# Merging the delta rule's block inverses in four steps of the pumped chain instead of one

## The chip, the cores and the metric

The kernel runs on one core of a Trainium2 chip. The metric is the device time of one execution in microseconds, the median of several runs. Five engines work side by side, each through its own queue in order: TensorE (PE in the profile; its weight loads are PEld), VectorE (DVE), ScalarE (ACT), GpSimd (POOL) and SyncE (SP), which here issues weight loads. A semaphore tells one engine that another is done.

## The reference, cut to what matters

A decoder trunk of two layers on x of 256 x 2048, fp32. Layer 0 is a gated DeltaNet with 16 heads of 128 x 128, layer 1 is differential attention; each ends with a squared-ReLU MLP, and each sub-layer with a layer norm. The part that the change touches is the chunked delta rule:

```python
lower = where(strict, einsum('bhnid,bhnjd->bhnij', k_beta, k) * decay, 0.0)
tri = lower + eye(CHUNK)
rhs = concatenate([v * beta, k_beta * exp(g)], -1)
sol = triangular_solve(tri, rhs, lower=True, unit_diagonal=True)
...
o = rms_norm(o, norm_w) * silu(z)
return o @ w_out
```

The kernel takes a chunk of 128 rows in place of 64, which gives the same function: two tiles t = 0, 1 of 128 rows for the 256 positions. Each (head, tile) has a triangular matrix of 128 x 128 whose inverse is applied to a right-hand side.

## The kernel before, in words

Nearly all of the time goes into gemms with streamed weights. `gemm` puts a gemm of 256 x K by K x 1024 into a plan; `run` goes through the plan in steps of SC = 4 weight tiles. In a step, for both row tiles t, every weight tile takes part in `product`: three 128x512 matmuls (L174, L175, L176) for high times high, high times low and low times high parts of fp32 numbers, for each of the two column groups. I call these the dense products; their tile is `acc`. `load_weights` fetches the tiles of the next step (L159, on SyncE's queue), and `split` makes the high part on ScalarE (L78) and the low part on VectorE (L79).

Small work is laid between the dense products. After each t of a step `pump` emits one item of the list `chain` and `rate` items (here 2) of the list `units`. `drain` empties both at once; the second gate gemm calls it at its last step, since the output projection behind it needs the whole delta rule. A scheduler then places the emitted instructions on the engines' queues by dependencies and buffers, so an engine's order is not quite the order of emission. Pools bound what can be under way: 11 buffers `blk` (128 x 2048), 8 buffers `sm` (128 x 512), and in PSUM 4 `acc` and 4 `ps`.

The delta rule runs in two halves of 8 heads. For each half there are gemms for k, q and v, then for both halves two gate gemms. Of a half:

- `score` (four items, two heads each): decay rows on VectorE (L525, L526), cumulative sums and k·k, q·k products on TensorE (L530 to L535, L550, L551), exponentials on ScalarE (L538, L539), causal selection on GpSimd (L541), products on VectorE (L553, L554). It leaves U1, A1 and UA2.
- the chain of `start_inverse`: `inv_gather` collects the 64 diagonal blocks of 32 x 32 through DRAM, three items that do nothing (rests), six items `inv_rows` with VectorE's forward substitution (L580, L587), `inv_scatter` (L589) sends the inverses back through DRAM into Z, two rests, `inv_flip` turns the blocks on VectorE (L601) into Y, a rest, and `inv_merge` (L603).
- `inv_merge` builds the inverse of 128 x 128 out of those of 32 x 32: for two 32-blocks at (0, 32) and at (64, 96), then for two 64-blocks, a lower product U·Z (L617), a copy on ScalarE (L618), the product with Y (L621) and a negated eviction to Y on VectorE (L622); for the first pair the turned product (L628) and an eviction to Z (L629) as well. A group is 16 matmuls of 32x32, or 8 of 64x64 for eight of the 16 matrices. All of it is one item of the chain.
- `solve` (two items, four heads each, put into the chain by `start_solve` when v is done): products with the inverse and U1 on TensorE (L642, L647, L651), copies on ScalarE (L643, L652), a subtraction on VectorE (L648), the output (L657, L659), its norm with small operations on VectorE (L665 to L671, `rsqrt` L85 to L89), and the scaled output `st["o"]` (L672).

The evacuation of a gate gemm, `ev` of `gate`, applies tanh on ScalarE, multiplies on VectorE (L738) and multiplies by `st["o"]` (L739); `to_features` then transposes it on TensorE (L204) as input of the output projection.

Of the kernel before, what the change touches and what calls it, by code (L numbers as in the profile page):

```python
# [14 lines left out]
ALU = mybir.AluOpType  # L15
# [3 lines left out]
P = 128  # L19
# [6 lines left out]
G = 512  # L26
# [9 lines left out]
class Trunk:  # L36
# [178 lines left out]
    @staticmethod  # L215
    def cols(w, c0, r0=0):
        return lambda k: w[r0 + k * P : r0 + (k + 1) * P, c0 : c0 + C]
# [96 lines left out]
    @staticmethod  # L314
    def ends(n):

        return [5, 5, 6] if n == D // C - 1 else None
# [47 lines left out]
    def gated_deltanet(self, x, w_in, conv_w, a_log, dt_bias, norm_w, w_out, g, b, out=None):  # L365
# [6 lines left out]
        nc = self.nc  # L372
        v_ = nc.vector
        NH, DK, HH = 16, 128, 8
# [198 lines left out]
        def inv_rows(hf, j0, j1):  # L573
            Gp = hf["inv"][:64, :C].rearrange("p (j i) -> p j i", j=32)
            X = hf["inv"][:64, C:].rearrange("p (i c) -> p i c", i=32)
            for j in range(j0, j1):
                n = 31 - j
                t0 = j % 2 * 256
                t = hf["t"][:64, t0 : t0 + n * (j + 1)].rearrange("p (i c) -> p i c", i=n)
                v_.tensor_tensor(  # L580
                    t,
                    Gp[:, j, j + 1 :].unsqueeze(2).broadcast_to([64, n, j + 1]),
                    X[:, j : j + 1, : j + 1].broadcast_to([64, n, j + 1]),
                    op=ALU.mult,
                )
                xs = X[:, j + 1 :, : j + 1]
                v_.tensor_tensor(xs, xs, t, op=ALU.subtract)  # L587

        def inv_scatter(hf):  # L589
            X = hf["inv"][:64, C:].rearrange("p (i c) -> p i c", i=32)  # L590
            hf["Z"] = self.blk()
            nc.gpsimd.memset(hf["Z"], 0.0)
            Zv = hf["Z"].rearrange("p (n c) -> p n c", c=P)
            buf = self.dram.tile([4, 2 * HH, 32, 32], F32, name="g_inverses")
# [4 lines left out]
        def inv_flip(hf):  # L599
            hf["Y"] = self.blk()  # L600
            v_.transpose(hf["Y"], hf["Z"])  # L601

        def inv_merge(hf):  # L603

            Z = hf["Z"].rearrange("p (n c) -> p n c", c=P)
            Y = hf["Y"].rearrange("p (n c) -> p n c", c=P)
            U = lambda n: hf["U1"][:, n] if n < HH else hf["UA2"][:, 0, n - HH]
            mm = nc.tensor.matmul
            for w, r0 in ((32, 0), (32, 64), (64, 0)):
                a, b_ = slice(r0, r0 + w), slice(r0 + w, r0 + 2 * w)  # L610
                per = G // w
                for n0 in range(0, 2 * HH, per):
                    N = range(n0, n0 + per)
                    cs = lambda n: slice((n - n0) * w, (n - n0 + 1) * w)
                    tp, ts = self.ps(), self.sm()
                    for n in N:
                        mm(tp[b_, cs(n)], U(n)[a, b_], Z[a, n, a], start=True, stop=True)  # L617
                    nc.scalar.copy(ts[b_], tp[b_])  # L618
                    yp = self.ps()
                    for n in N:  # L620
                        mm(yp[a, cs(n)], ts[b_, cs(n)], Y[b_, n, b_], start=True, stop=True)  # L621
                    v_.tensor_scalar(  # L622
                        Y[a, n0 : n0 + per, b_], yp[a].rearrange("p (n c) -> p n c", c=w), -1.0, None, op0=ALU.mult
                    )
                    if w == 32 and r0 == 0:
                        zp = self.ps()
                        for n in N:
                            mm(zp[b_, cs(n)], Y[b_, n, b_], ts[b_, cs(n)], start=True, stop=True)  # L628
                        v_.tensor_scalar(  # L629
                            Z[b_, n0 : n0 + per, a], zp[b_].rearrange("p (n c) -> p n c", c=w), -1.0, None, op0=ALU.mult  # L630
                        )

        def solve(hf, gi, H):

            Y = hf["Y"].rearrange("p (n c) -> p n c", c=P)
            rv = hf["r"]
# [39 lines left out]
        def start_inverse(hf):  # L676
            rest = [(lambda *a: None, (hf,))]
            rows = [(lambda hf, j=j: inv_rows(hf, j, min(j + 6, 31)), (hf,)) for j in range(0, 31, 6)]
            self.chain.extend([(inv_gather, (hf,))] + rest * 3 + rows)
            self.chain.extend([(inv_scatter, (hf,))] + rest * 2 + [(inv_flip, (hf,))] + rest + [(inv_merge, (hf,))])  # L680

        def start_solve(hf, H):
            self.chain.extend((solve, (hf, g_, H)) for g_ in range(NG))
# [1 line left out]
        def half(hh):  # L685
            hf, H = {}, hh * HH

            def ev_for(name, ct):
# [15 lines left out]
                def follow():  # L704
                    if name == "v":
                        hf["r"] = self.blk().rearrange("p (t h d) -> p t h d", t=NT, h=HH)
                        for h in range(0, HH, 2):
                            self.later(v_unit, hf["raw"], h, ct, hf["r"], hf["rsc"])
                        if hh == 0:
                            st["o"] = [self.blk() for _ in range(NT)]  # L710
                        self.later(start_solve, hf, H)
                        return
                    hf[name] = self.blk().rearrange("p (h t) -> p h t", h=HH)
                    hf["S" + name] = self.small([NT, HH], "g_S" + name)
                    for h in range(0, HH, 2):
                        self.later(qk_unit, hf["raw"], h, ct, hf[name], hf["S" + name])
                    if name == "q":
                        self.later(scalars, hf, H)
                        for h in range(0, HH, 2):
                            self.later(score, hf, H, h)  # L720
                        self.later(start_inverse, hf)
# [232 lines left out]
```

## Time and profile before

| | us |
|---|---|
| median of 3 runs | 2472.16 |
| lowest and highest run | 2465.31, 2475.14 |
| profiled execution | 2465.03 |
| its span | 2463.3 |
| TensorE busy | 2416.1 (98%) |
| VectorE busy | 1497.2 (61%) |
| ScalarE busy | 1078.2 (44%) |
| GpSimd busy | 90.3 (4%) |
| mean granted clock of TensorE | 0.992 |

The profile is of one execution; L12 is line 12 of the kernel. Times in it are microseconds from the start of the span. A row of the timeline gives start, length, engine, line, operation, output and inputs, size and count, and in brackets how long the engine stood idle ahead of it and for whom. A view by stretches gives busy time and number of records of each engine in each stretch and the TensorE clock that was granted, 1.00 being full. Matmuls overlap, so what one takes from the next is the distance of two starts; an fp32 matmul outside the dense products makes two records.

### The profile page before, as it was taken

How to read it: one execution, taken by the hardware profiler on the slowest of the kernel's cores; microseconds unless marked ns; L12 is line 12 of the kernel's file. 1: busy time of each engine (PE TensorE's matmuls, PEld its weight loads, DVE VectorE, ACT ScalarE, POOL GpSimd, SP SyncE). 2: the span in 40 equal slices, each digit the busy share in tenths (PEclk: the TensorE clock that was granted, in tenths of full speed). 3: DMA queues.
4: the chain of work that ended last, by engine and by line, in shares of the span. 5: the costliest groups of instructions: out<-in, count | busy, mean ns of one | idle time of the engine just before them, and what ended most of it. 6: DMA issues, size and time to landing. Idle time of an engine off the chain costs nothing.

```text
span 2463.3 us, 30465 instructions
## 1 busy us (share of the span) xinstructions
PE 2416.1 (98%) x11492; PEld 1983.3 (81%) x11492; DVE 1497.2 (61%) x2333; ACT 1078.2 (44%) x1474; POOL 90.3 (4%) x94
## 2 busy tenths in 40 slices
PE   8999999998999999999998999999999999999997
PEld 7888888887888888888887878788788888888886
DVE  4789689667554544545557575665755554555556
ACT  4545345433443433434433464643443443443442
POOL 0010010002000000000002000000200000000001
PEclk9999899999999999999999999999999999999999
DMA  6545345564555556565554545455455555656553
GB/s 229 155 139 175 98 140 160 166 233 158 188 185 191 182 194 222 172 214 182 195 197 146 180 137 171 155 174 167 161 198 195 182 190 186 217 179 214 185 195 121
DMA packets 120211, 438.84 MB, mean 178 GB/s; under 512 B 13760, under 2 KB 13792, under 8 KB 119040
## 3 DMA queue, kind: packets, MB, share of 16 engines
q1 hardware_dynamic: 115920, 420.79, 52.0%
q0 software_dynamic: 2560, 11.13, 1.4%
q10 hardware_dynamic: 1584, 4.98, 0.5%
q8 instruction: 90, 1.47, 0.2%
q14 instruction: 57, 0.47, 0.1%
HBM read 433.70 MB, written 3.15 MB: 177 GB/s over the span
## 4 chain that ended last, share of the span: by engine, by line
PE 90%; DVE 6%; DMA 2%; issue 1%; ACT 1%; POOL 0%; ACTq 0%; POOLq 0%; DVEq 0%
PE acc L174 27%; PE acc L175 27%; PE acc L176 27%; PE ps L204 3%; DVE wl L79 1%; DVE blk L266 1%; DVE blk L265 1%; PE ps L819 1%; ACT wh L78 1%; PE ps L550 1%; DMA wr<-in_gdn_w_in_dram 1%; PE ps L485 1%; DMA wr<-in_mlp_w_up_dram 0%; PE ps L621 0%; PE ps L847 0%
## 5 line engine op out<-in xcount | busy, mean ns | idle before, releaser
L79 DVE TENSOR_TENSOR wl<-wr,wh 128x1024 fp32r<-128x1024 f32 x785 | 954.5, 1227 | 675.0 <-ACT wh L78 632.1
L78 ACT CAST wh<-wr 128x1024 fp32r<-128x1024 f32 x800 | 832.1, 1052 | 945.6 <-PE acc L176 757.2
L174 PE MATMUL acc<-wh,xhl 128*128 128x512 f32 x1920 | 764.3, 398 | 0.0
L175 PE MATMUL acc<-wl,xhl 128*128 128x512 f32 x1920 | 757.7, 395 | 3.2 <-POOL wl L79 3.2
L176 PE MATMUL acc<-wh,xhl 128*128 128x512 f32 x1920 | 754.8, 393 | 0.0
L174 PE MATMUL acc<-wh,blk 128*128 128x512 f32 x1280 | 500.0, 391 | 0.0
L176 PE MATMUL acc<-wh,blk 128*128 128x512 f32 x1280 | 499.4, 390 | 0.0
L175 PE MATMUL acc<-wl,blk 128*128 128x512 f32 x1280 | 499.1, 390 | 0.0
L175 PEld LDWEIGHTS acc<-wl,xhl 128*128 128x128 f32 x1920 | 363.7, 189 | 75.7 <-POOL wl L79 4.4
L174 PEld LDWEIGHTS acc<-wh,xhl 128*128 128x128 f32 x1920 | 363.8, 189 | 73.8 <-issue 1.7
L176 PEld LDWEIGHTS acc<-wh,xhl 128*128 128x128 f32 x1920 | 362.7, 189 | 73.9
L176 PEld LDWEIGHTS acc<-wh,blk 128*128 128x128 f32 x1280 | 240.4, 188 | 50.1
L174 PEld LDWEIGHTS acc<-wh,blk 128*128 128x128 f32 x1280 | 240.4, 188 | 49.5
L175 PEld LDWEIGHTS acc<-wl,blk 128*128 128x128 f32 x1280 | 240.5, 188 | 49.2
L293 DVE SCALAR_TENSOR_TENSOR blk<-blk,acc 128x512 f32<-128x512 f32 x80 | 54.7, 685 | 85.2 <-PE acc L176 85.2
L204 PE MATMUL ps<-ident,sm 128*128 128x128 f32 x512 | 81.3, 275 | 2.5 <-DVE sm L869 1.8
L204 PEld LDWEIGHTS ps<-ident,sm 128*128 128x128 f32 x512 | 61.3, 140 | 27.3 <-PE acc L176 7.1
L78 ACT CAST blk<-ps 128x512 fp32r<-128x512 f32 x80 | 46.8, 585 | 70.9 <-PE ps L204 70.9
L347 DVE TENSOR_TENSOR sm<-sm 128x512 f32<-128x512 f32 x64 | 44.0, 691 | 52.6 <-ACT sm L346 52.2
L79 DVE TENSOR_TENSOR blk<-ps,blk 128x512 fp32r<-128x512 f32 x80 | 55.0, 688 | 30.1 <-ACT blk L78 30.1
L346 ACT ACTIVATE sm<-acc 128x512 f32<-128x512 f32 x64 | 38.2, 597 | 65.4 <-PE acc L176 62.4
L471 DVE SCALAR_TENSOR_TENSOR sm<-blk,g_cw,sm 128x255 f32<-128x255 f32 (+2 forms) x144 | 60.8, 474 | 0.0
(202 smaller groups left out, 1049.7 us busy)
## 6 DMA issues: line engine op xcount, KB each, us to landing
wr<-in_mlp_w_up_dram SPq DMA_DIRECT2D x256, 512.0 KB, 4.7
wr<-in_mlp_w_down_dram SPq DMA_DIRECT2D x256, 512.0 KB, 5.2
wr<-in_gdn_w_in_dram SPq DMA_DIRECT2D x128, 512.0 KB, 4.4
wr<-in_shared_w_kv_dram SPq DMA_DIRECT2D x64, 512.0 KB, 5.1
wr<-in_gdn_w_out_dram SPq DMA_DIRECT2D x32, 512.0 KB, 5.4
wr<-in_diff_w_q_dram SPq DMA_DIRECT2D x32, 512.0 KB, 4.6
wr<-in_diff_w_o_dram SPq DMA_DIRECT2D x32, 512.0 KB, 4.7
blk<-in_ln_g_dram POOLq DMA_DIRECT2D x4, 1024.0 KB, 7.2
```

Of the source, the lines that this page charges most:

```text
L78: self.nc.scalar.copy(hi, src)
L79: (engine or self.nc.vector).tensor_tensor(lo, src, hi.bitcast(F32), op=ALU.subtract)
L174: mm(ps, xh, wh[:, c], start=(k == 0), stop=False)
L175: mm(ps, xh, wl[:, c], start=False, stop=False)
L176: self.last = mm(ps, xl, wh[:, c], start=False, stop=(k == nk - 1))
L204: self.nc.tensor.transpose(pt[:, i], src[:, i * P : (i + 1) * P], self.ident)
L265: v.scalar_tensor_tensor(xc, xc, ln["mv", t][:, 0:1], ln["g"][:, c], op0=ALU.subtract, op1=ALU.mult)
L266: v.scalar_tensor_tensor(xc, xc, ln["rs", t], ln["b"][:, c], op0=ALU.mult, op1=ALU.add)
L293: self.nc.vector.scalar_tensor_tensor(rc, rc, alpha, ps, op0=ALU.mult, op1=ALU.add)
L346: self.nc.scalar.activation(a, ps, AF.Relu)
L347: self.nc.vector.tensor_tensor(a, a, a, op=ALU.mult)
L471: v_.scalar_tensor_tensor(y[:, i, d:], u[:, : T - d], w(j), y[:, i, d:], op0=ALU.mult, op1=ALU.add)
```

## The change

The arithmetic of the merge stays, and so does the number of its matmuls, copies and evictions. It is cut into `lower`, `upper` and `turned`, and `merge_steps` lists them in four steps: both lower products of the 32-blocks; the upper and turned products of the 32-blocks; the lower products of the 64-blocks; their upper products. Each step is an item of the chain of its own, so the chain of a half is three items longer, and the solves, which stand behind it, come three pumps later. The copies `ts` are kept from one step to the next.

```diff
-        def inv_merge(hf):
...
-            for w, r0 in ((32, 0), (32, 64), (64, 0)):
-                a, b_ = slice(r0, r0 + w), slice(r0 + w, r0 + 2 * w)
-                per = G // w
-                for n0 in range(0, 2 * HH, per):
...
-                        mm(tp[b_, cs(n)], U(n)[a, b_], Z[a, n, a], start=True, stop=True)
-                    nc.scalar.copy(ts[b_], tp[b_])
...
-                        mm(yp[a, cs(n)], ts[b_, cs(n)], Y[b_, n, b_], start=True, stop=True)
...
-                            mm(zp[b_, cs(n)], Y[b_, n, b_], ts[b_, cs(n)], start=True, stop=True)
...
+            def lower(w, r0, n0):
+                a, b_ = ends(w, r0)
+                tp, ts = self.ps(), self.sm()
+                for n in range(n0, n0 + G // w):
+                    mm(tp[b_, cols(w, n0, n)], U(n)[a, b_], Z(n)[a, a], start=True, stop=True)
+                nc.scalar.copy(ts[b_], tp[b_])
+                hf["ts", w, r0, n0] = ts
...
+            return [
+                [(lower, 32, 0, 0), (lower, 32, 64, 0)],
+                [(upper, 32, 0, 0), (turned, 32, 0, 0), (upper, 32, 64, 0)],
+                [(lower, 64, 0, 0), (lower, 64, 0, HH)],
+                [(upper, 64, 0, 0), (upper, 64, 0, HH)],
+            ]
+
+        def inv_merge(hf, i):
+            for fn, *args in merge_steps(hf)[i]:
+                fn(*args)
...
-            self.chain.extend([(inv_scatter, (hf,))] + rest * 2 + [(inv_flip, (hf,))] + rest + [(inv_merge, (hf,))])
+            self.chain.extend([(inv_scatter, (hf,))] + rest * 2 + [(inv_flip, (hf,))] + rest + [(inv_merge, (hf, i)) for i in range(4)])
```

In the changed file lines behind the merge lie 23 lower: L623 is the lower product, L635 the upper, L642 the turned one; L665, L670, L674, L680 and L682 are the solve's products (L642, L647, L651, L657, L659 before).

What the scheduler makes of it is seen in TensorE's order. First the merge of half 0, before: L617 is a lower group, L621 an upper, L628 the turned one, and rows of `acc` are dense products.

```order
L617 MATMUL ps<-blk 32x32 x16
L175 MATMUL acc<-wl,xhl 128x512
L176 MATMUL acc<-wh,xhl 128x512
L175 MATMUL acc<-wl,xhl 128x512
L176 MATMUL acc<-wh,xhl 128x512
L175 MATMUL acc<-wl,xhl 128x512
L621 MATMUL ps<-blk,sm 32x32 x16
L628 MATMUL ps<-sm,blk 32x32 x16
L617 MATMUL ps<-blk 32x32 x16
```

The same place after, L623 being the lower, L635 the upper and L642 the turned groups; the dense row at the end is the first of 17, behind which the lower group of 64x64 stands.

```order
L623 MATMUL ps<-blk 32x32 x32
L175 MATMUL acc<-wl,xhl 128x512
L176 MATMUL acc<-wh,xhl 128x512
L175 MATMUL acc<-wl,xhl 128x512
L176 MATMUL acc<-wh,xhl 128x512
L635 MATMUL ps<-blk,sm 32x32 x16
L642 MATMUL ps<-sm,blk 32x32 x16
L635 MATMUL ps<-blk,sm 32x32 x16
L175 MATMUL acc<-wl,xhl 128x512
```

Both lower groups now stand together, and the three groups that use them follow four dense products later.

Second, on TensorE again, the passage from the first to the second score of half 1, before (L550 and L551 are a score's k·k and q·k products, L530 and L534 the first of the next score):

```order
L550 MATMUL ps<-blk 128x256
L551 MATMUL ps<-blk 128x128
L176 MATMUL acc<-wh,xhl 128x512
L174 MATMUL acc<-wh,xhl 128x512
L175 MATMUL acc<-wl,xhl 128x512
...
L175 MATMUL acc<-wl,xhl 128x512
L176 MATMUL acc<-wh,xhl 128x512
L530 MATMUL ps<-sm,g_after 128x512
L534 MATMUL ps<-sm,g_after 128x256
```

After, from the second score to the third:

```order
L550 MATMUL ps<-blk 128x256
L551 MATMUL ps<-blk 128x128
L530 MATMUL ps<-sm,g_after 128x512
L534 MATMUL ps<-sm,g_after 128x256
L550 MATMUL ps<-blk 128x256
L551 MATMUL ps<-blk 128x128
```

Ten dense products stood between the scores; between the second, third and fourth none is left, and eight lie behind the first.

Third, the end of half 1 on TensorE, before: the second solve, from its first products (L642) to its output (L657).

```order
L642 MATMUL ps<-blk 128x128 x4
L176 MATMUL acc<-wh,xhl 128x512
L174 MATMUL acc<-wh,xhl 128x512
L175 MATMUL acc<-wl,xhl 128x512
L176 MATMUL acc<-wh,xhl 128x512
L647 MATMUL ps<-blk 128x128 x4
...
L651 MATMUL ps<-blk 128x128 x4
L657 MATMUL ps<-blk 128x128 x5
```

After, from the last product of the first solve (L682):

```order
L682 MATMUL ps<-blk 128x128
L665 MATMUL ps<-blk 128x128 x4
L670 MATMUL ps<-blk 128x128 x4
L674 MATMUL ps<-blk 128x128 x4
L680 MATMUL ps<-blk 128x128 x5
```

The ten dense products inside the second solve have moved to places ahead of it; behind it stand nine, and then the first transposes (L204) of the gated output.

More of the change, by code (lines that the diff above doesn't have):

```diff
@@ L601, in inv_flip, with merge_steps @@
             v_.transpose(hf["Y"], hf["Z"])
-        def inv_merge(hf):
-            Z = hf["Z"].rearrange("p (n c) -> p n c", c=P)
-            Y = hf["Y"].rearrange("p (n c) -> p n c", c=P)
+        def merge_steps(hf):
+            mm = nc.tensor.matmul
+            Z = lambda n: hf["Z"][:, n * P : (n + 1) * P]
+            Y = lambda n: hf["Y"][:, n * P : (n + 1) * P]
             U = lambda n: hf["U1"][:, n] if n < HH else hf["UA2"][:, 0, n - HH]
-            mm = nc.tensor.matmul
-            for w, r0 in ((32, 0), (32, 64), (64, 0)):
-                a, b_ = slice(r0, r0 + w), slice(r0 + w, r0 + 2 * w)
-                per = G // w
-                for n0 in range(0, 2 * HH, per):
[L613 to L617, printed above, removed]
-                    nc.scalar.copy(ts[b_], tp[b_])
[L619 to L627, printed above, removed]
-                            mm(zp[b_, cs(n)], Y[b_, n, b_], ts[b_, cs(n)], start=True, stop=True)
-                        v_.tensor_scalar(
-                            Z[b_, n0 : n0 + per, a], zp[b_].rearrange("p (n c) -> p n c", c=w), -1.0, None, op0=ALU.mult
-                        )
@@ new lines, in ends, with cols @@
+            def ends(w, r0):
+                return slice(r0, r0 + w), slice(r0 + w, r0 + 2 * w)
+            def cols(w, n0, n):
+                return slice((n - n0) * w, (n - n0 + 1) * w)
+            def lower(w, r0, n0):
[5 more added lines that the diff above has]
+                hf["ts", w, r0, n0] = ts
@@ new lines, in negated, with upper @@
+            def negated(dst, rows, cs, w, n0, ps):
+                d = dst.rearrange("p (n c) -> p n c", c=P)[rows, n0 : n0 + G // w, cs]
+                v_.tensor_scalar(d, ps[rows].rearrange("p (n c) -> p n c", c=w), -1.0, None, op0=ALU.mult)
+            def upper(w, r0, n0):
+                a, b_ = ends(w, r0)
+                ts, yp = hf["ts", w, r0, n0], self.ps()
+                for n in range(n0, n0 + G // w):
+                    mm(yp[a, cols(w, n0, n)], ts[b_, cols(w, n0, n)], Y(n)[b_, b_], start=True, stop=True)
+                negated(hf["Y"], a, b_, w, n0, yp)
@@ new lines, in turned @@
+            def turned(w, r0, n0):
+                a, b_ = ends(w, r0)
+                ts, zp = hf["ts", w, r0, n0], self.ps()
+                for n in range(n0, n0 + G // w):
+                    mm(zp[b_, cols(w, n0, n)], Y(n)[b_, b_], ts[b_, cols(w, n0, n)], start=True, stop=True)
+                negated(hf["Z"], b_, a, w, n0, zp)
+            return [
[4 more added lines that the diff above has]
+            ]
```

## The prediction

> **What bounds the kernel now.** I read the page first, then the waits of TensorE around the delta rule, then the clock by stretches, then single instructions. The page's first lines give the span, TensorE's busy time, and the granted clock in 40 slices:
>
> ```profile
> span 2463.3 us, 30465 instructions
> PE 2416.1 (98%) x11492; PEld 1983.3 (81%) x11492; DVE 1497.2 (61%) x2333; ACT 1078.2 (44%) x1474; POOL 90.3 (4%) x94
> PEclk9999899999999999999999999999999999999999
> PE 90%; DVE 6%; DMA 2%; issue 1%; ACT 1%; POOL 0%; ACTq 0%; POOLq 0%; DVEq 0%
> ```
>
> TensorE is busy for 98% and carries 90% of the chain that ended last. The change keeps every matmul, so it can act in two ways only: through the time in which TensorE waits, and through its clock. The waits of TensorE from 200 to 520 us, where both halves of the delta rule lie (us in total, times, longest):
>
> ```profile
> PE ps L617 <- DMA blk<-g_inverses: 1.7, 1, 1.7
> PE ps L204 <- DVE sm L739: 0.5, 1, 0.5
> PE ps L485 <- ACT sm L479: 0.3, 1, 0.3
> ```
>
> 2.5 us of waits in 320: there is little to win there, and much that can get worse. The clock has more. The fifth slice above is an 8. These are stretches (us from the start, then length, TensorE busy and records, ..., granted clock, DMA share, GB/s) around the merge of half 0 (first two), in the merge of half 1 (third), and at two boundaries of layers:
>
> ```profile
> 264.50:267.90 3.40, 3.40 (x99) 3.25 (x99) 2.63 (x4) 0.27 (x1) 0.00 (x0) 1.00 0.94 290
> 268.00:288.40 20.40, 20.40 (x128) 16.32 (x127) 5.63 (x6) 5.09 (x7) 0.00 (x0) 0.50 0.32 96
> 455.70:459.10 3.40, 3.40 (x84) 2.93 (x83) 3.00 (x3) 1.29 (x2) 0.00 (x0) 1.00 0.28 76
> 1312.40:1315.80 3.40, 1.42 (x5) 0.86 (x5) 3.23 (x9) 0.00 (x0) 0.67 (x1) 1.00 0.69 211
> 1315.80:1319.20 3.40, 2.89 (x11) 2.51 (x12) 2.68 (x5) 1.17 (x2) 0.00 (x0) 0.51 0.11 45
> 602.50:605.90 3.40, 1.59 (x9) 1.44 (x10) 3.40 (x4) 0.82 (x2) 1.12 (x1) 1.00 0.25 101
> ```
>
> Half 0's merge runs for 20.4 us at half clock, which loses 10.2 us; half 1's merge keeps its clock. Cold time comes in pieces of about 3.4 us: one at 1315.8, six behind 268. So one piece costs 1.7 us. Of those stretches, the same view for the dense products (tile acc) alone gives:
>
> ```profile
> 264.50:267.90 3.40, 0.52 (x3) 0.34 (x3) 0.00 (x0) 0.00 (x0) 1.00 0.94 290
> 455.70:459.10 3.40, 1.19 (x6) 0.65 (x4) 0.00 (x0) 0.00 (x0) 1.00 0.28 76
> ```
>
> The stretch ahead of the loss has TensorE busy for all of its 3.40 us, but only 0.52 us of that in 128x512 products; the rest are 32x32 matmuls. In half 1 it was 1.19 us, and the clock held. I read from it that 32x32 matmuls count for little in what holds the clock, and that the point lies somewhere between those two amounts.
>
> [...]
>
> **The change part by part.** *Half 0's merge.* The rows that I use for durations (start, length, line, shapes):
>
> ```profile
> 263.79 0.39 PE L175 MATMUL acc<-wl,xhl 128*128 128x512 f32 x1
> 264.02 0.40 PE L176 MATMUL acc<-wh,xhl 128*128 128x512 f32 x1
> 264.57 1.10 PE L621 MATMUL ps<-blk,sm 32*32 32x32 f32 x29
> 267.52 0.50 PE L176 MATMUL acc<-wh,xhl 128*128 128x512 f32 x1
> 271.62 0.63 PE L175 MATMUL acc<-wl,xhl 128*128 128x512 f32 x1
> 272.04 0.63 PE L176 MATMUL acc<-wh,xhl 128*128 128x512 f32 x1
> ```
>
> A dense product takes 0.23 us warm (263.79 to 264.02) and 0.42 cold. The three groups of 16 small matmuls between 264.57 and 267.52 take 2.95 us. After the change two groups (about 2 us) come first, then four dense products (0.9 us), then three groups (2.95 us): 6 us that hold 0.9 us of dense work. That is thinner than before, and I expect the clock to fall here again. But then 17 dense products stand in a row (3.9 us warm, 7.1 cold), and 24 behind the first 64x64 group, where before 64x64 groups and solves came every few products. So it should come back after one or two pieces, not six. I take two, 3.4 us; from 0 (no fall) to 10.2 (six, as before). Net −6.8 us, from −10.2 to 0.
>
> *The solves and the scores of half 1.* The chain is three items longer, so each solve is emitted three pumps later. VectorE then takes the scores of half 1 behind the solves' small operations, and in TensorE's order scores two, three and four follow one another without a dense product between them. The selections of two scores on GpSimd, TensorE's first and last row of a score, and VectorE's first eviction of a score and its first two decay rows, in before:
>
> ```profile
> 349.09 0.84 POOL L541 TENSOR_SCALAR_AFFINE_SELECT sm<-sm 128x256 f32<-128x256 f32 x2 [5.48 <-ACT sm L538]
> 355.17 0.77 POOL L541 TENSOR_SCALAR_AFFINE_SELECT sm<-sm 128x256 f32<-128x256 f32 x2 [5.24 <-ACT sm L538]
> 346.99 0.39 PE L530 MATMUL ps<-sm,g_after 128*128 128x512 f32 x1
> 350.31 0.39 PE L551 MATMUL ps<-blk 128*128 128x128 f32 x2
> 343.29 0.48 DVE L553 SCALAR_TENSOR_TENSOR blk<-ps,g_c,sm 128x256 f32<-128x256 f32 x1 [0.30 <-POOL sm L541]
> 345.90 0.35 DVE L525 TENSOR_SCALAR sm<-mask,g_g 128x256 fp32r<-128x256 f32 x1
> 346.35 0.35 DVE L525 TENSOR_SCALAR sm<-mask,g_g 128x256 fp32r<-128x256 f32 x1
> ```
>
> A score came every 6.1 us, of which TensorE's own part is about 3.5 (346.99 to the end of the last pair); ten or more dense products filled the rest. Without them VectorE sets the pace: eight evictions from 343.29 to 345.90 (2.6 us) and four pairs of decay rows at 0.45 (1.8) make 4.4 us a score, 0.9 more than TensorE has to do. With a weight subtraction (L79, about 1.2 us) between them it is 5.6. Two such gaps make 1.8 to 4.2 us; at the old period of 6.1 and with a late VectorE, up to 9; nothing, if VectorE gets ahead. I take 3.5, nearer to the 4.2, since two weight subtractions do stand among these scores in VectorE's order.
>
> *The end of half 1.* The drain at the last step of the second gate gemm empties what is left of the chain. Three items later, more is left, and the order shows the second solve right behind the first, with no dense product among its parts, and then nine dense products ahead of the transposes (L204) of the gated output. Before:
>
> ```profile
> 473.90 1.28 PE L657 MATMUL ps<-blk 128*128 128x128 f32 x10
> 476.58 1.06 PE L642 MATMUL ps<-blk 128*128 128x128 f32 x8
> 477.39 0.48 PE L176 MATMUL acc<-wh,xhl 128*128 128x512 f32 x1
> 480.85 1.09 PE L651 MATMUL ps<-blk 128*128 128x128 f32 x8
> 481.77 1.28 PE L657 MATMUL ps<-blk 128*128 128x128 f32 x10
> 484.37 0.48 PE L174 MATMUL acc<-wh,xhl 128*128 128x512 f32 x1
> 489.23 0.63 PE L204 MATMUL ps<-ident,sm 128*128 128x128 f32 x4
> 480.04 0.68 DVE L648 TENSOR_TENSOR blk<-blk,ps 128x512 f32<-128x512 f32 x1
> ```
>
> From the first solve's output (473.90) to the second solve's third product (480.85) lie 6.95 us, set by VectorE: L648 is queued behind the first solve's square roots and ends just ahead of 480.85. TensorE's own part of that is 2.7 us (473.90 to 476.58), 0.8 (476.58 to 477.39) and one more group at 0.9 (480.85 to 481.77), 4.4 together; the ten dense products that filled the other 2.5 us are gone, so 2.5 us idle. The gated output needs the last square roots too: 4.86 us from 484.37 to 489.23, of which nine products cover 2.05, so 2.8 idle. Sum 5.3; from 3, if some dense work slips in, to 9, if each of the later transposes waits as well.
>
> *Half 1's merge.* Its first groups are apart (13 and 15 dense products between), but behind them 48 + 32 + 32 small matmuls have only 4 + 3 dense ones among them: about 9 us with 1.6 us of dense work. The 48 alone are the group that lost the clock in half 0. One cold piece, 1.7 us; from 0 to 8.5 (five).
>
> *Idle gaps.* 1.98 us idle in one piece (1312.4) were followed by a cold one, 1.81 (602.5) were not. The stalls above reach that size at two places. One cold piece, 1.7 us; 0 to 5. [...]
>
> *Without a price.* The inverse's wait for its scatter, 1.7 us, stays: the rows of the inverse stand later in VectorE's order by more weight subtractions, but so does the first merge group in TensorE's. Cover gone would cost up to 3 us; finished early it gains 1.7. Evictions are as many as before. The two copies that a step leaves for the next hold two of the eight sm buffers for a pump longer; nothing around them waited for such a buffer in the list above, so I cost it at nothing (up to one wait like L204's, 0.5). SyncE's order of weight loads is unchanged. On GpSimd's queue the load of head_w comes ahead of the layer norm's rows, which are used much later.
>
> *Sum.* 2465.03 (the profiled execution) − 10.2 + 3.4 + 3.5 + 5.3 + 1.7 + 1.7 = 2470.4. The median of 2472.16 lies 7.1 above that execution; half of this, 3.5, is my share for where a middle run stands: 2473.9, so **2474 us**. No gain, though the half clock of half 0 goes for the most part: the drain and the scores give it back.
>
> **The rivals.**
>
> *A, slower: the clock falls in both merges for long.* In half 0 the 6 us with 0.9 us of dense work end in a cold piece, and since cold products take 0.42 us and the groups twice as long, the gate sees thin stretches again: six pieces, 6.8 us over my sum. In half 1 the bunch at the drain does the same for five pieces instead of one, 6.8 more. 2474 + 13.6 = 2488. It decides from a piece with less dense work than between 0.52 and 1.19 us. For it: the fall in before came from just this group. Against it: dense runs of 17 and 24 products. 0.27.
>
> *B, faster: spreading works as it sounds.* No cold piece anywhere (−3.4 − 1.7 − 1.7), VectorE ahead at the scores (−3.5), and at the drain only the lower end (−2.3): 2474 − 12.6 = 2461; with the timing at the profiled execution's level (−3.5) 2458. 0.13.
>
> *C, the gate holds as long as TensorE is busy.* No cold piece in the merges, stalls as I have them: 2474 − 3.4 − 1.7 = 2469. [...] 0.10.
>
> *D, it does not spread.* The scheduler orders by itself, and in half 0 the groups already stood apart; six cold pieces stay in half 0 and the rest is as I have it: 2474 + 6.8 = 2481. 0.15.
>
> **How the numbers follow.** My forecast has 0.35 (its own range 2464 to 2484). A measurement of this kernel can tell about 0.5% from no change, 12.4 us, so faster is under 2459.8 and slower over 2484.5. A lies over it; B lies at the lower bound, and half of it falls short; some of the forecast's own low tail goes below. Faster 0.13, the same 0.60, slower 0.27. The range, 2460 to 2490, leaves out half of B and the upper part of A.
>
> **What would show it.** In the profile after: granted clock over half 0's merge, two cold pieces instead of six; waits of TensorE for VectorE's decay rows or GpSimd's selections at three of half 1's scores; waits at the second solve's third product and at the first gated transposes. No cold piece and no new waits would prove me wrong on the fast side; a cold stretch of over 15 us in either merge on the slow side.

## The result, and the profile after

The changed kernel takes 2486.03 us (median of 6 runs, 2484.26 to 2489.67) against 2467.27 us of the kernel before, now from 6 runs (2459.43 to 2475.14). The ratio is 1.0075, 95% interval 1.0053 to 1.0097: slower by three quarters of a per cent. The profiled execution took 2484.43 us. Its page gives the span, TensorE's busy time and the granted clock in 40 slices:

```profile
span 2482.6 us, 30455 instructions
PE 2420.5 (98%) x11492; PEld 1983.7 (80%) x11492; DVE 1496.3 (60%) x2333; ACT 1078.4 (43%) x1474; POOL 89.8 (4%) x94
PEclk9999999999999999999999999999999999999999
```

The 8 in the fifth slice has gone, and the span is 19.3 us longer nevertheless. The waits of TensorE around the delta rule, in the stretch from 200 to 560 us (us in total, times, longest), say where a good part of it is; before there were three rows with 2.5 us:

```profile
PE ps L530 <- DVE sm L525: 4.7, 3, 1.9
PE ps L623 <- DMA blk<-g_inverses: 4.0, 1, 4.0
PE acc L174 <- DVE sm L761: 2.8, 1, 2.8
PE ps L674 <- DVE blk L671: 1.9, 2, 1.2
PE acc L175 <- DVE wl L79: 1.4, 3, 1.0
PE ps L204 <- DVE sm L762: 1.2, 1, 1.2
PE ps L670 <- ACT blk L666: 0.8, 1, 0.8
PE ps L204 <- DVE sm L474: 0.7, 1, 0.7
PE ps L485 <- ACT sm L479: 0.5, 1, 0.5
```

That makes 18.0 us, 15.5 more than before. The first row is the scores of half 1, the second the inverse's transfer in half 1, and rows three, four and seven are half 1's solves and the gated output behind them. The clock in the same execution, by stretches (length, TensorE busy, ..., granted clock, DMA share, GB/s):

```profile
264.00:274.20 10.20, 10.20 (x120) 8.65 (x117) 4.01 (x5) 0.93 (x3) 0.00 (x0) 0.50 0.50 174
465.40:468.80 3.40, 3.40 (x9) 2.71 (x9) 0.78 (x1) 0.58 (x1) 0.00 (x0) 0.50 0.72 194
503.00:506.40 3.40, 3.18 (x8) 2.53 (x9) 3.40 (x13) 0.60 (x2) 0.00 (x0) 0.50 0.00 0
608.80:612.20 3.40, 3.40 (x11) 2.82 (x12) 2.94 (x5) 1.03 (x2) 0.00 (x0) 0.50 0.03 5
622.40:625.80 3.40, 3.40 (x11) 2.75 (x10) 3.40 (x5) 1.64 (x2) 0.00 (x0) 0.51 0.34 67
```

Half 0's merge has three cold pieces where there were six. One is new behind the transfer's wait (465), one behind the gated output's wait (503), and two at a boundary of layers where before had none.

Both traces hold 9600 dense products, and each stretch of the table below holds as many of each line in both (41 products have changed places with others of their stretch), so the time can be laid between products of the same number. For each stretch: its length in both, TensorE's idle time, and half of its cold time (the granted clock was 0.50 in it, 0.51 in the last stretch above), which I put down as what the clock cost there.

| dense products | what lies there | before: length, idle, clock | after: length, idle, clock | difference |
|---|---|---|---|---|
| 0 to 840 | half 0 up to its merge | 237.4, 0.3, 0 | 237.9, 0.6, 0 | +0.4 |
| 840 to 1260 | half 0's merge and solves, half 1's scores | 152.9, 0.0, 10.2 | 154.1, 5.5, 5.1 | +1.2 |
| 1260 to 1440 | half 1's inverse | 43.4, 0.5, 0 | 45.6, 1.6, 0 | +2.2 |
| 1440 to 1620 | half 1's merge and solves, gated output | 66.4, 1.8, 0 | 78.8, 10.5, 3.4 | +12.4 |
| 1800 to 2000 | boundary of layers | 56.7, 6.2, 0 | 60.1, 6.6, 3.4 | +3.4 |
| all others | | 1881.4, 15.6, 5.1 | 1881.4, 14.9, 5.1 | 0.0 |

So the gain of 5.1 us on half 0's clock is used up by 5.5 us of waits in the same stretch, and most of the loss arises 200 us later, at the end of half 1. Over the whole table TensorE's idle time rises by some 15 us and the clock's cost by 1.7; the rest, not quite 3 of some 19.5 us, is spread over the stretches and is in neither.

One execution tells little of the clock, since it differs between executions of one kernel (mean granted clock 0.985 to 0.996 over 65 runs of the kernel before). Every run, profiled or not, lists span and mean granted clock, and span times mean clock is my estimate of what the run would have taken at full clock, if TensorE works at half pace through all of its cold time (in the changed kernel's profile dense products start 0.23 us apart ahead of half 0's merge and 0.43 us apart in the cold stretch at 264); what it idles there is booked by half as a loss of the clock. For the kernel before the product is 2443.4 us (mean of 18 runs; 2444.1 and 2443.1 in the two later sets of 20 and 27), while its clock losses go from 9.8 to 37.2 us. One more run of the first of these sets, 6713.28 us in the slow state, is left out throughout. This splits the loss without a trace: the changed kernel is at 2461.4, so 18.0 us do not come from the clock, and it loses 23.2 us to the clock against 22.1 of before (mean of the 65 runs), 1 us. Below, "at full clock" is this product, and a difference in it is put beside the one in time.

### The profile page after: what moved, and what is told of

The parts are those of the page before. It is cut to its first block, busy times and chain, and to the rows that moved or that the text cites. A ratio compares the mean times of both kernels' runs of the same rounds, so it can differ in the third digit from the quotient of the medians.

```text
span 2482.6 us, 30455 instructions
## 1 busy us (share of the span) xinstructions
PE 2420.5 (98%) x11492; PEld 1983.7 (80%) x11492; DVE 1496.3 (60%) x2333; ACT 1078.4 (43%) x1474; POOL 89.8 (4%) x94
## 4 chain that ended last, share of the span: by engine, by line
PE 88%; DVE 7%; DMA 2%; issue 1%; ACT 1%; POOL 0%; ACTq 0%; DVEq 0%; POOLq 0%; SPq 0%
PE acc L174 27%; PE acc L175 27%; PE acc L176 27%; PE ps L204 3%; DVE wl L79 2%; DVE blk L266 1%; DMA wr<-in_gdn_w_in_dram 1%; PE ps L842 1%; DVE blk L265 1%; ACT wh L78 1%; PE ps L485 1%; DMA wr<-in_mlp_w_up_dram 0%; PE ps L870 0%; PE ps L550 0%; PE ps L635 0%
## 5 line engine op out<-in xcount | busy, mean ns | idle before, releaser
L204 PE MATMUL ps<-ident,sm 128*128 128x128 f32 x512 | 81.0, 275 | 3.5 <-DVE sm L892 1.2
L204 PEld LDWEIGHTS ps<-ident,sm 128*128 128x128 f32 x512 | 61.3, 140 | 27.7 <-PE acc L176 6.7
```

The lines of the kernel that those rows point to most:

```text
L204: self.nc.tensor.transpose(pt[:, i], src[:, i * P : (i + 1) * P], self.ident)
```

## The experiments

Theory 1: the loss comes from half 0's solves being three pumps later; they push half 1's scores back on VectorE, and all behind them is late. Theory 2: it comes from the bunched groups of the merge. Theory 3: it comes from half 1's own steps, which the drain empties at once. Four kernels tell them apart.

**The delay alone.** Against the kernel before:

```diff
-... + rest + [(inv_merge, (hf,))])
+... + rest + [(inv_merge, (hf,))] + rest * 3)
```

> The merge stays in one item of the chain, in the old order, and three items that do nothing are put behind it, so that the solves come three pumps later as in the changed kernel. Theory 1 (the loss comes from half 0's solves being later: they run into half 1's scores on VectorE, which makes half 1's inverse and all behind it late): waits of about 5 us at the scores, 8 to 9 us more at the end of half 1, half 0's merge cold for six pieces as before; 12 to 22 us slower than the kernel before. Theory 2 (the loss comes from the merge's groups being bunched, through the clock and through waits within the merge): no difference over 3 us. Theory 3 (the loss comes from half 1's own steps, which the drain empties at once): no difference over 3 us.

2493.02 us, ratio 1.0114 (1.0066 to 1.0161); 2462.5 at full clock, 19 us more than the kernel before. The first four of its nine rows of waits from 200 to 560 us:

```profile
PE ps L530 <- DVE sm L525: 4.3, 3, 1.9
PE ps L617 <- DMA blk<-g_inverses: 3.1, 1, 3.1
PE ps L651 <- DVE blk L648: 2.8, 2, 1.6
PE acc L174 <- DVE sm L738: 2.8, 1, 2.8
```

The same rows as in the changed kernel, with the merge untouched. In this profile half 0's merge was cold for six pieces again. These are theory 1's places, and at full clock its size; by time the ratio makes 28 us, more than its 12 to 22, most of the excess being clock (28.0 us of losses in these four runs against 21.8). Theories 2 and 3 expected nothing.

**Four steps in one half only.** Against the changed kernel, in the end of `start_inverse` (the second kernel has `> 0`):

```diff
+            if hf["H"] == 0:
+                self.chain.extend((inv_merge, (hf, i)) for i in range(4))
+            else:
+                self.chain.append((inv_merge, (hf, 4)))
```

where step 4 is all of the merge in the old order.

> Half 0's merge in four steps, half 1's in one item and the old order. Theory 1: 12 to 20 us slower than the kernel before, with the waits at the scores and at the end of half 1 all there, since only half 0's solves need be late for them; three cold pieces in half 0 in place of six. Theory 2: about half of the loss, 5 to 10 us slower. Theory 3: the same time or up to 5 us faster (three cold pieces fewer).

2491.29 us, ratio 1.0114 (1.0062 to 1.0165), 2461.2 at full clock: the whole loss (by time again more than expected, with 29.3 us of clock losses), and it lies in the same places (4.3 us at the scores; 11.7 us idle between products 1440 and 1620), although half 1's code is the old one.

> Half 0's merge in one item and the old order, half 1's in four steps. Theory 1: within 5 us of the kernel before, no waits at the scores, the inverse of half 1 as early as before. Theory 2: 5 to 10 us slower. Theory 3: 8 to 12 us slower, the waits at the end of half 1 being there without the late scores.

2460.98 us, ratio 0.9978 (0.9956 to 1.0001), 2443.6 at full clock. Its waits from 200 to 560 us, complete, and its clock where the kernel before was cold:

```profile
PE ps L623 <- DMA blk<-g_inverses: 2.3, 1, 2.3
PE ps L485 <- ACT sm L479: 0.8, 1, 0.8
```

```profile
264.50:285.00 20.50, 20.50 (x267) 17.36 (x266) 9.76 (x13) 7.19 (x16) 0.00 (x0) 1.00 0.51 159
```

Half 1's steps cost nothing, and the drain that empties the last of them at once costs nothing: theory 3 falls. What it gains in time is clock, 16.5 us of losses against 21.8. The clock's row was not expected by any theory: half 0 has the very instructions of the kernel before here, and no cold piece.

**The changed order, without the delay.** All four steps in one item:

```diff
-            for fn, *args in merge_steps(hf)[i]:
+            for fn, *args in sum(merge_steps(hf), []):
```

with one `inv_merge` in the chain.

> The four steps' instructions in the changed kernel's order, but all in one item of the chain in both halves, so that nothing behind them is later. Theory 1: within 5 us of the kernel before; rather faster (5 us) if half 0 has three cold pieces here too. Theory 2: 10 to 19 us slower. Theory 3: within 5 us.

2461.56 us, ratio 0.9985 (0.9964 to 1.0005), 2442.9 at full clock. The bunched groups cost nothing: theory 2 falls. Its profile has three cold pieces in half 0, so three in place of six belong to the order of the groups, not to the steps' being spread:

```profile
265.00:275.20 10.20, 10.20 (x108) 8.54 (x109) 3.52 (x5) 1.50 (x2) 0.00 (x0) 0.50 0.47 157
```

The next question was whether the loss is one, handed on from the scores, or two.

**Two pumps later, and one.** `rest * 2` in place of `rest * 3`; and the changed kernel with its steps in pairs, so that the solves come one pump later:

```diff
-            for fn, *args in merge_steps(hf)[i]:
+            for fn, *args in merge_steps(hf)[2 * i] + merge_steps(hf)[2 * i + 1]:
```

> The merge in one item and the old order, and two idle items behind it in place of three: the solves come two pumps later than in the kernel before. In TensorE's order the scores of half 1 have 10 to 14 dense products between them again, but the end of half 1 has its second solve without any, as in the changed kernel. Theory 1a (two separate losses, each where the dense products have run out: at the scores, and at the end of the second gate gemm): no waits at the scores, 8 to 10 us of waits at the end of half 1; 8 to 14 us slower than the kernel before. Theory 1b (one loss, the late scores, which everything behind them inherits): half of the full loss or less at both places, 3 to 8 us. Theory 3' (the loss grows with each pump of delay): two thirds, about 12 us, shared by both places.

2481.82 us, ratio 1.0067 (1.0046 to 1.0087), 2456.1 at full clock, 12.0 us more than the kernel before. The longest of its waits from 200 to 560 us, where no row of L530 stands:

```profile
PE ps L617 <- DMA blk<-g_inverses: 4.7, 1, 4.7
PE ps L651 <- DVE blk L648: 2.8, 2, 1.6
PE acc L174 <- DVE sm L738: 2.8, 1, 2.8
```

The scores wait for nothing, and the end of half 1 has its full loss (12.8 us idle between products 1440 and 1620). So they are two losses, as theory 1a has it: at full clock inside its 8 to 14 us, by time (16.5 us by the ratio) above them.

> The merge in two items of the chain (steps one and two, steps three and four), so that the solves come one pump later. The order has dense products between the scores and in both solves of half 1. Theories 1a and 1b: within 5 us of the kernel before, rather faster, as the two kernels of the first series without a delay. Theory 3' (a loss for each pump): a third, 6 us slower.

2464.56 us, ratio 0.9995 (0.9976 to 1.0014), 2444.7 at full clock. At full clock one pump costs under 1 us, two cost 12, three 18 to 19: not so much for each pump.

**What the end of half 1 needs.** Half 0 stays as before; in half 1 alone two idle items more, then six, ahead of the inverse's rows; and the changed kernel with one fewer there:

```diff
-            self.chain.extend([(inv_gather, (hf,))] + rest * 3 + rows)
+            self.chain.extend([(inv_gather, (hf,))] + rest * (5 if hf["H"] else 3) + rows)
```

(9 for six more; 2 in the changed kernel.)

> Half 0 as before. In half 1 alone two idle items more stand between the gather and the rows of the inverse, so that its merge begins some 39 dense products later, about as late as in the changed kernel, while the scores stay where they were. In TensorE's order the solves still have 4 to 6 dense products among their parts. Theory 1a: what counts is whether dense products are left to cover the solves, not how late they are: within 5 us of the kernel before. Theory 1b (lateness of half 1's inverse itself costs): 8 us slower or more.

2462.15 us, ratio 0.9993 (0.9968 to 1.0019), 2441.1 at full clock: 3.0 us less than the kernel before in the same series (2444.1), of which the wait for the inverse's transfer, 1.7 us in the profile before and absent here, makes the larger part. By time the two cannot be told apart.

> Half 0 and the scores as before; in half 1 alone six idle items more ahead of the inverse's rows. Merge and solves of half 1 all come when the second gate gemm has no dense product left. Theory 1a: the end of half 1 waits for 10 to 25 us, more than in the changed kernel since the merge is bare as well; 10 to 25 us slower than the kernel before, with nothing changed in half 0. If the end of half 1 were not what counts: within 5 us.

2492.49 us, ratio 1.0099 (1.0072 to 1.0127). Its two longest waits from 200 to 560 us, and its clock behind the merge's start:

```profile
PE ps L621 <- DVE blk L601: 7.3, 1, 7.3
PE acc L174 <- DVE sm L739: 2.8, 1, 2.8
```

```profile
469.50:503.60 34.10, 23.93 (x235) 22.68 (x236) 7.95 (x13) 4.06 (x14) 0.00 (x0) 0.50 0.17 53
```

With merge and solves bare, TensorE is idle for 10.2 of 34.1 us and cold for all of it. 2453.1 at full clock and 37.7 us of clock losses, against 2443.1 and 22.9 of the kernel before in the same series: 10.0 and 14.8 more. By this profile 5.1 us of the clock's 14.8 are idle time in that cold stretch, booked by half, so that waits cost some 15 us and the clock some 10.

> The changed kernel with one of the three idle items behind the gather taken out of half 1's chain alone. Its scores are as late as in the changed kernel (the same order, no dense products between them), but the first solve of half 1 begins 22 dense products before the second gate gemm runs out of them, in place of 9, and both solves have 4 to 6 dense products among their parts again. Theory 1a (two separate losses, each where the dense products have run out): the waits at the scores stay (4 to 6 us), those at the end of half 1 go down to 4 us or less; 5 to 9 us slower than the kernel before in place of 18. Theory 1b (late scores cost at the end whatever the cover): 15 to 20 us slower still.

2481.30 us, ratio 1.0057 (1.0037 to 1.0077), 2453.8 at full clock. Its waits from 200 to 560 us begin with

```profile
PE ps L530 <- DVE sm L525: 4.7, 3, 1.9
PE acc L175 <- DVE wl L79: 3.2, 2, 1.8
PE ps L623 <- DMA blk<-g_inverses: 1.9, 1, 1.9
PE acc L174 <- DVE sm L762: 1.6, 1, 1.6
```

The scores wait as in the changed kernel; idle time between products 1440 and 1620 is 3.5 us in place of 10.5, though the scores are just as late. So the late scores alone do not make the loss at the end, as theory 1b would have it. At full clock 10.7 us are left of 18.0, a little over what was expected: between products 1260 and 1440 idle time is 4.3 us in place of 1.6, mostly for weight subtractions on VectorE. By time this is a miss: the ratio makes 14 us, not 5 to 9, and its interval overlaps that of the changed kernel, so that the gain is seen in the waits and at full clock and not in the time. The clock takes 26.8 us, against 22.9 of the kernel before in the same series, and the profile has four cold pieces from half 1's merge on:

```profile
474.60:478.00 3.40, 3.40 (x99) 3.19 (x98) 1.53 (x3) 0.00 (x0) 0.00 (x0) 1.00 0.09 35
478.00:491.70 13.70, 13.70 (x83) 11.61 (x83) 1.89 (x3) 1.75 (x3) 0.00 (x0) 0.50 0.01 2
```

The first of these stretches holds the group of 48 small matmuls and 0.53 us of dense products.

The count that orders these kernels is how many dense products of the second gate gemm are left in TensorE's order when half 1's first solve begins:

| kernel | products left | idle us, products 1440 to 1620 |
|---|---|---|
| late_inverse_six | 0 | 18.5 |
| delay_two | 1 | 12.8 |
| delay_alone | 1 | 12.6 |
| half0_in_steps | 1 | 11.7 |
| changed kernel | 9 | 10.5 |
| half1_one_less | 22 | 3.5 |
| late_inverse | 27 | 0.6 |
| order_and_late (below) | 32 | 0.1 |
| two_steps | 40 | 3.4 |
| before | 42 | 1.8 |
| half1_in_steps | 42 | 2.3 |
| order_alone | 47 | 3.2 |

From 22 on the waits are 3.5 us or less, and what is left of them is mostly the inverse's transfer; from 9 down they are 10 us and more. No kernel lies between 9 and 22.

**The clock by itself.** The kernel before with two runs of matmuls that nothing uses, behind the gathers of the two halves:

```diff
+        def small_run(hf):
+            p, o = self.ps(), self.sm()
+            w, n = (32, 128) if hf["H"] == 0 else (128, 36)
+            for i in range(n):
+                c = i % (G // w)
+                nc.tensor.matmul(p[:w, c * w : (c + 1) * w], self.ident[:w, :w], self.mask[:w, :w], start=True, stop=True)
+            nc.scalar.copy(o[:w], p[:w])
```

> The kernel before with extra work that nothing uses: behind the gather of half 0 a run of 128 matmuls of 32x32, behind that of half 1 a run of 36 matmuls of 128x128, each about 8 us with TensorE busy throughout and no dense product inside. If 32x32 matmuls count for little in what holds the clock: one or two cold pieces of 3.4 us behind the first run and none behind the second. If only the busy time of TensorE counts: none behind either.

One run, 2491.43 us with the extra work. Two stretches of the run of 32x32, then two of the run of 128x128:

```profile
174.80:178.20 3.40, 3.40 (x113) 3.40 (x111) 0.00 (x0) 0.39 (x1) 2.07 (x4) 1.00 0.26 53
178.30:188.50 10.20, 10.20 (x148) 9.45 (x145) 0.00 (x0) 0.57 (x1) 2.35 (x2) 0.50 0.11 27
...
383.60:387.00 3.40, 3.40 (x33) 3.40 (x32) 0.00 (x0) 0.00 (x0) 0.54 (x1) 1.00 0.29 72
387.00:390.40 3.40, 3.40 (x23) 2.98 (x23) 0.00 (x0) 1.03 (x2) 2.16 (x3) 1.00 0.04 10
```

TensorE is busy throughout both. After 3.4 us of 32x32 matmuls the clock falls, and it stays down for three pieces (one or two were expected): the rest of that run, 7.4 us, and 2.8 us behind it. With 128x128 it holds through the run and behind it (1.00 in both rows). The first row shows TensorE busy for 3.40 of 3.40 us, and the second a granted clock of 0.50 behind it, so the busy time that a profile shows did not decide here.

**A kernel that beats both.** The order of the steps in one item (`order_alone`) and two idle items more in half 1 (`late_inverse`):

> The two kernels of which I expect most, together: all merge steps in one item of the chain in the changed order, and two idle items more ahead of half 1's rows, so that TensorE does not wait for the inverse's transfer. At full clock this should take about 3 us less than the kernel before (the transfer's wait gone, no other), and with the clock losses of the other two kernels (17 to 22 us as against 22) it should come out 3 to 8 us faster than the kernel before, a ratio of 0.997 to 0.999.

2458.23 us (12 runs), ratio 0.9958 (0.9940 to 0.9977), against 1.0075 of the changed kernel. Two lines of its page, and its waits from 200 to 560 us, complete:

```profile
span 2455.3 us, 30465 instructions
PEclk9999999999999999999999999999999999999999
```

```profile
PE ps L485 <- ACT sm L479: 1.3, 1, 1.3
PE ps L204 <- DVE sm L763: 0.2, 1, 0.2
```

2441.4 us at full clock, 1.7 less than before where 3 were expected, and 15.4 us of clock losses against 22.9 in the same series: the gain is clear, and most of it is clock.

## Why the prediction was right or wrong

The measured 2486.03 lies inside the range (2460 to 2490). The middle, 2474 and no change, does not hold: the kernel is slower, a case that had 0.27. By the medians it loses 18.8 us where 2 were forecast, and that the range held is owed to its width of 30 us.

*Waits and clock as the only two ways.* Right for most of it: some 15 us of idle time and 1.7 of clock out of 19.5 in the two profiles, 18 outside the clock and 1 by it over the runs.

*Half 0's clock, −10.2 + 3.4.* Here the sum failed. Three pieces came instead of two, but that is 1.7 us; the mistake was to take the six pieces of one execution for the kernel's own price. With the old order in half 0, four of seven profiles have six pieces (before, delay_alone, clock_small, late_inverse_six) and three have none (half1_in_steps, delay_two, late_inverse): 5.9 us on average, at 1.7 for a piece. With the new order four of six have three (the changed kernel, half0_in_steps, order_alone, half1_one_less) and two have none: 3.4. On these profiles the term is some −2.4 us, not −6.8, and in the changed kernel's profile new falls elsewhere cost 6.8.

*The scores, 3.5 (0 to 9).* 4.7 us in three waits. The range held, and VectorE does set the pace. The first rows of scores two to four after the change:

```profile
357.74 0.51 PE L530 MATMUL ps<-sm,g_after 128*128 128x512 f32 x1 [0.88 <-DVE sm L525]
363.85 0.50 PE L530 MATMUL ps<-sm,g_after 128*128 128x512 f32 x1 [1.89 <-DVE sm L525]
369.82 0.50 PE L530 MATMUL ps<-sm,g_after 128*128 128x512 f32 x1 [1.90 <-DVE sm L525]
```

6.1 and 6.0 us from one to the next. The stretch between VectorE's first decay rows of the last two (length, TensorE, weight loads, VectorE busy, ...), and VectorE's first eviction in it:

```profile
363.45:369.42 5.97, 4.06 (x22) 3.44 (x22) 5.67 (x19) 0.87 (x2) 0.79 (x2) 1.00 0.29 88
366.81 0.48 DVE L553 SCALAR_TENSOR_TENSOR blk<-ps,g_c,sm 128x256 f32<-128x256 f32 x1 [0.30 <-POOL sm L541]
```

VectorE works for 5.67 of 5.97 us, a weight subtraction among it: the 5.6 of the prediction. The two gaps that it counted make 3.8 us, against 3.5; the third, 0.88 ahead of the second score, was not in the sum. VectorE's idle 0.3 us is a wait for GpSimd's selection, so a score goes round a loop: TensorE, the exponential, the selection, VectorE's evictions, and behind those in VectorE's queue the next score's decay rows. The period of 6.1 us that the prediction gives for the kernel before comes from one pair of selections; by the first rows of its scores (L530 at 339.99, 346.99, 352.83 and 360.25) it was 7.0, 5.8 and 7.4 us, with 12, 10 and 16 dense products between.

*The end of half 1, 5.3 (3 to 9).* Idle time between products 1440 and 1620 rose by 8.7. The places were right:

```profile
488.70 1.16 PE L674 MATMUL ps<-blk 128*128 128x128 f32 x8 [0.70 <-DVE blk L671]
494.24 1.16 PE L670 MATMUL ps<-blk 128*128 128x128 f32 x8 [0.82 <-ACT blk L666]
496.57 1.16 PE L674 MATMUL ps<-blk 128*128 128x128 f32 x8 [1.17 <-DVE blk L671]
503.22 0.80 PE L174 MATMUL acc<-wh,blk 128*128 128x512 f32 x1 [2.81 <-DVE sm L761]
```

The second solve waits for 0.82 + 1.17 = 2.0 us (2.5 forecast), the gated output for 2.81 (2.8 forecast; it is shown at the next accumulation, which waits for the evacuation, and not at the transposes). The rest is what I had put at nothing: the inverse's transfer, 4.0 us in place of 1.7 ("Cover gone would cost up to 3 us", against 2.3 here), the first solve's 0.70, and 1.0 for a weight subtraction.

*One cold piece at half 1's merge, one behind an idle gap.* Two came, at 465 and 503, so the 3.4 us are right, but for the merge by luck: the piece at 465 begins behind 4.0 us of waiting for the inverse's transfer, ahead of the thin part of the merge. That part kept its clock: the piece from 475.6 has the group of 48 and 1.20 us of dense products. In half1_one_less the same group fell into a piece with 0.53 us of them, and the clock was lost. Both fit the reading of the prediction, lost at 0.52 and held at 1.19. Two more at the boundary of layers, 3.4 us, were not foreseen; the kernel before has none there in its one profile, but every other profile has one to three.

*The cause.* The prediction named both places, and did not see that one thing makes both: the delay of half 0's solves. It treated half 1's drain as if half 1's own three items counted; half1_in_steps shows that they don't.

*The rivals.* ("The gate" in A and C is whatever grants TensorE its clock; the runs show the granted clock alone.) A has about the right time, 2488, by a mechanism that did not act: its clock loss is 1 us. B needed VectorE ahead at the scores, and it was behind. C, that the clock holds as long as TensorE is busy, falls with the run of 32x32 matmuls: 3.40 of 3.40 us busy, then a clock of 0.50. D falls with its six cold pieces, since three came; it is right in that spreading is not what made them fewer, as order_alone has three as well.

What stays open: by which step the delay of half 0's solves makes half 1's inverse late even where the scores wait for nothing (delay_two). Scores begin 36 dense products later in its order and the merge 43. From the last score to the first merge group its order has 341 dense products, the changed kernel 340, the kernel before 335: the inverse seems to follow the scores at a fixed distance, so that late scores would make it late without any wait. The orders show this, no run isolates it.

## What to carry to other kernels

Cutting a piece of background work into more items costs its followers a pump each, and a follower may be far away: look in the new order for where the filler runs out, a chain that found 22 or more filler products left waited for 3.5 us or less here, one that found 9 or fewer for over 10. Compare kernels by span times mean granted clock as well as by time, and look in the trace for idle time in cold stretches, which this product counts by half: the standard deviation of the kernel before is 5.8 us by time and 1.6 by that product (65 runs). And a cold stretch in one profile is one draw (with the old order half 0's merge was cold in four of seven profiles); price it over several executions.

## What the runs showed of the hardware

The granted clock changed on a grid of 3.41 us. In the profiles of the kernel before and of the changed kernel, the shortest cold stretch is 3.41 us, and the times of any two changes inside the span lie a whole multiple of that apart; the cold stretches shown here, 3.4, 10.2, 13.7, 20.4 and 34.1 us, are one, three, four, six and ten of it. From the span's start, the grid's points lie 0.49 us earlier in the changed kernel's profile than in that of the kernel before (first points at 14.87 and 15.36 us). In the 13 profiles here, whether half 0's merge went cold went with its place on that grid. Measured as the time from a grid point to the dense product behind the first merge group: with the old order 2.10 (the kernel before), 2.37, 2.59 and 2.72 us in the four profiles with six pieces, 0.04, 0.16 and 1.39 in the three with none. With the new order it is 0.02, 0.43 (the changed kernel), 2.35 and 3.30 for three pieces, 1.51 and 1.56 for none.

Once lost in a stretch of small matmuls, the clock stayed lost with TensorE fully busy: 20.4 us in the kernel before, and 10.2 in clock_small, of which the run of 32x32 fills the first 7.4.
